# A stick-breaking attention layer with a SwiGLU FFN: first-stage and attention orders joined, two x blocks loaded a projection sooner, xn by tiles, first FFN casts reordered

## The chip, the cores and the metric

The kernel runs on one core of a Trainium2 chip. The metric is device time in microseconds (us) for one launch, taken as the median of several runs. The core has a matmul engine (TensorE, PE in the profile, with its weight loads as PEld), VectorE (DVE), ScalarE (ACT), GpSimd (POOL) and SyncE (SP), which here issues the DMA transfers. Each engine works through its own queue in order. Matmuls write into PSUM, which has eight banks of 128 × 512 float32; everything else lies in SBUF.

## What is computed

One transformer layer, S = 2048 tokens, D = 1024, 16 heads of 64, all float32: a stick-breaking attention, then a SwiGLU feed-forward network. Both are wrapped in RMS norms with shift, scale and gate that come from a conditioning vector c.

```python
mod_all = einsum('bd,lde->lbe', silu(c), ada_w) + ada_b[:, None]
sh_m, sc_m, gt_m, sh_f, sc_f, gt_f = split(mod_all[i][:, None, :], 6, axis=-1)
h = rms_norm(x, norm_g[i, 0]) * (1 + sc_m) + sh_m
q, k, v = heads(h @ w_qkv)
for q0 in range(0, s, 128):                      # stick-breaking attention
    z = einsum('bthd,bshd->bhts', q[:, q0:q0+128], k[:, :q0+128]) * 64 ** -0.5
    sp = where(mask, softplus(z), 0.0)
    a = exp(where(mask, z - cumsum(sp, axis=3, reverse=True), -inf))
    o = einsum('bhts,bshd->bthd', a, v[:, :q0+128])
x = x + gt_m * rms_norm(o @ w_o, norm_g[i, 1])
h = rms_norm(x, norm_g[i, 2]) * (1 + sc_f) + sh_f
g, u = split(h @ ffn_w_in, 2, axis=-1)
x = x + gt_f * rms_norm((silu(g) * u) @ ffn_w_out, norm_g[i, 3])
```

## The kernel before

**Matmuls.** A float32 product is made of three fp32r matmuls on high and low halves: each operand is cast (`high`), the rest is subtracted (`low`), and `mm3` (L160 to L162) adds three of the four products of halves into the same PSUM tile. So every operand needs a cast and a subtraction on other engines before PE may use it, and a tile of h or of a weight appears in the profile as two operations (`ht` with L722 or L348 the cast, L727 or L350 the low half).

**Blocks.** Tokens go in four blocks of 512 (indices 0 to 3; "token blocks 3 and 4" are indices 2 and 3), channels of D in eight slices k of 128 (KC = 8), heads in eight pairs p. A projection step (p, b) makes the keys, queries and values of one pair for one block: three products of eight slices each, in the order t = 1 (keys), 0 (queries), 2 (values). `STEPS` lists the steps; (1, 0) is pulled to the second place and its results are parked in memory (`k_park`, `q_park`, `v_park`), so that the list begins (0, 0), (1, 0), (0, 1), (0, 2), (0, 3). `project` is a generator: it yields after each slice, and the attention slots (scores z, the scan w, the transposes t, the outputs o) are emitted between the slices. After a product, `split` makes high and low of the result (`kn`, `qn`), and SP stores them to the layouts kt and qt that the scores read.

**First stage (0 to about 50 us).** Block 0's norm needs shift and scale of the first norm, columns of silu(c) @ ada_w. For each quarter q of two channel slices, DVE adds up weight rows (`ada_sum`, tile `asum`, L656 and L659), PE multiplies two of the rows itself (`ada_direct`, L669) and then the sum (`ada_rest`, L676), all into columns of one PSUM tile `acol`; `ada_cols_done` (L684 to L687) makes `shift` and `g_eff` on DVE. Then the transposed tiles xT (`x_turn`, L332) are modulated on ACT (L718), cast (L722), their low half taken on DVE (`low`, L727), and three products (keys, queries, values of step (0, 0)) take them slice by slice (`first_products`). The weights w0, w1, w2 of step (0, 0) are cast on ACT (`weights_high`, L697), their low halves made on DVE (`weights_low`, L702).

**x of the other blocks.** Blocks 1 to 3 are loaded by `x_load` (four tiles of 128 tokens, L314), squared on ACT with the mean on DVE and the power on POOL (`x_square`), scaled on DVE into `xn` (`x_scale`, L323), transposed (L332) and modulated slice by slice in `first_norm`. For blocks 2 and 3 the load is emitted at the first slice of the key product of the step just before the block's own. All four squares come at slices 0 to 3 of the following query product, all four scales at slices 4 to 7. Three transposed tiles follow at slices 2, 4 and 6 of the value product, and the other five in the block's own key product. Block 0 and 1 take a PSUM bank of the pool `tps` for xT, blocks 2 and 3 one of the three banks of `accps`, in which the projections' accumulators (`pj`), the turned values (`vt`) and the late modulation's columns (`ap`) rotate. A tile takes the next bank and waits until the tile that had it before is read.

**Late modulation.** `late_modulation` for segments 2, 3 and 4 (the attention's gate, shift and scale of the second norm) runs beside the attention, a little per slot: loads, sums on DVE, then a tile `ap` from `accps`, matmuls (L230, L283) and a result on DVE (L238, L297).

**FFN.** Its two products are done by a scheme with seven block products, whose operands are sums of blocks with high and low halves of their own. `FIRST_AT` says at which product of the first group which left and right operands are split (`left_split`, `right_split`); these casts run on ACT ahead of or behind the copies of the products (L1329).

Of the kernel before, what the change touches and what calls it, by code (L numbers as in the profile page):

```python
# [9 lines left out]
F32 = mybir.dt.float32  # L10
F32R = mybir.dt.float32r
AF = mybir.ActivationFunctionType
ALU = mybir.AluOpType
# [3 lines left out]
P = 128  # L17
D = 1024
S = 2048
KC = D // P  # L20
# [71 lines left out]
def hybrid_trunk_kernel(  # L92
# [83 lines left out]
    def sb(shape, dtype, **kw):  # L176

        return (odd if kw["tag"] in ODD_TAGS else att).tile(shape, dtype, **kw)
# [66 lines left out]
            g_eff[:, which, ks], sc, 1.0, gc[:, which, ks], op0=ALU.add, op1=ALU.mult  # L245
        )

    def late_modulation(segs, tag, n, ahead, waits, pool, ptag, acc_tag="tmp", rows_tag="wraw", settle=3, pace=1):

        chunks = [(seg, half, k0) for seg in segs for half in range(2) for k0 in range(0, KC, n)]  # L250
        loaded = []

        def load():
            if len(loaded) < len(chunks):
                loaded.append(ada_load(*chunks[len(loaded)], n, tag, BUFS[tag]))

        for _ in range(ahead):
            load()
        for at, (seg, half, k0) in enumerate(chunks):
            if ahead == 0 or at == 0:  # L260
# [12 lines left out]
            if k0 + n < KC:  # L273
                continue
            for _ in range(settle):
                yield
            ps = pool.tile([P, BT], F32, name=f"ap{seg}_{half}", tag=ptag)
            if seg in (2, 5):
                g = seg // 3
                rows = sb([P, 2, BT], F32, name=f"gr{g}_{half}", tag=rows_tag, bufs=BUFS[rows_tag])  # L280
                nc.sync.dma_start(rows, gate_consts[g : g + 1, half].to_broadcast((P, 2, BT)))
                if seg == 2:
                    nc.tensor.matmul(ps, ones, acc, start=True, stop=True)  # L283
# [38 lines left out]
    def x_scale(b, i):  # L322
        nc.vector.tensor_scalar(  # L323
            x_norm[b, i], x_tiles.pop((b, i)), x_rstd.pop((b, i)), None, op0=ALU.mult
        )

    def x_turn(b, k):

        pool, tag = (tps, "t") if b < 2 else (accps, "acc")
        pt = pool.tile([P, BT], F32, name=f"xT{b}_{k}", tag=tag)  # L330
        for i in range(4):
            nc.tensor.transpose(  # L332
                pt[:, i * P : (i + 1) * P], x_norm[b, i][:, k * P : (k + 1) * P], ident
            )
        return pt
# [22 lines left out]
        return h  # L358

    norm_h, norm_tile = {0: []}, {}  # L360

    def first_norm(b, k):
        if b is None or k >= KC:
# [29 lines left out]
    def project(at):  # L393
# [3 lines left out]
        early, parked = (p, b) in EARLY, (p, b) == PARKED  # L397

        nb = STEPS[at + 1][1] if at + 1 < len(STEPS) and STEPS[at + 1][0] == 0 else None
        if STEPS[at] == (PARKED[0], 1):  # L400
            unpark()
        h = norm_h[b] if p == 0 or parked else h_load(p, b)

        def product(t):
            if begun:
                return first_acc[t]
            w = weights[p, t]
            if parked and t == 1:
                acc = zps.tile([P, BT], F32, name=f"pj{p}_{b}_{t}", tag="z")
            else:  # L410
                acc = accps.tile([P, BT], F32, name=f"pj{p}_{b}_{t}", tag="acc")
            ahead = b == NB - 1 and p + 1 < NPAIR
            for k in range(KC):
                if t == 1:
                    if p == 0:
                        first_norm(b, k + 3)
                    if k == 0 and nb and nb > 1:
                        x_load(nb)
                    if k == 5 and waiting:
                        waiting.pop()()  # L420
                if parked and t == 1 and k % 2 == 0:
                    nc.sync.dma_start(*stores[k // 2])
                if parked and (t, k) == (1, 6):
                    split_early(1, 2, ["whl"])
                if t == 0 and nb:
                    (x_square if k < 4 else x_scale)(nb, k % 4)
                if t == 2 and k in (2, 4, 6):
                    first_norm(nb, k // 2 - 1)
                if ahead and k == 0:
                    load_weights(p + 1, t)  # L430
                if ahead and k == 6:
                    split_weights(p + 1, t)
                mm3(acc, (w[0][:, k], w[1][:, k]), (h[k][:, 0], h[k][:, 1]), k == 0, k == KC - 1)
                yield
            return acc

# [208 lines left out]
            chunks[q, k] = w[:, :, k % 4]  # L645

    def ada_begin(q):
        cols_ps[q] = zps.tile([P, BT], F32, name=f"acol{q}", tag="z")
        nc.vector.memset(cols_ps[q][:, :4], 0.0)

    def ada_sum(q, k):
        w, scale = chunks[q, k], c_act[:, k : k + 1]
# [13 lines left out]
    def ada_direct(q, k):  # L666

        for n, seg, js in COLUMNS:
            nc.tensor.matmul(  # L669
                cols_ps[q][:, n : n + 1], chunks[q, k][:, seg, js], c_act[:, k : k + 1],  # L670
                start=False, stop=False, skip_group_check=True,
            )

    def ada_rest(q):
        for n, seg, js in COLUMNS:
            nc.tensor.matmul(  # L676
                cols_ps[q][:, n : n + 1], piece_sums[q][:, seg, js], ones[:, 0:1],
                start=False, stop=n == 3, skip_group_check=True,
            )

    def ada_cols_done(q):

        ps, ms = cols_ps.pop(q), slice(2 * q, 2 * q + 2)
        nc.vector.tensor_tensor(shift[:, 0, ms], ps[:, 0:2], b_cols[:, 0, ms], op=ALU.add)  # L684
        sc = sb([P, KC], F32, name=f"sc0_{q}", tag="sc", bufs=1)[:, :2]
        nc.vector.tensor_tensor(sc, ps[:, 2:4], b_cols[:, 1, ms], op=ALU.add)
# [78 lines left out]
    ada_direct(0, 0)  # L765
    turned_x = {m: x_turn(0, m) for m in range(2)}
    ada_direct(0, KC - 1)
    ada_rest(0)
    weights_high(1)
    weights_low(1)  # L770
    ada_cols_done(0)
    weights_high(0)
    weights_low(0)
    weights_high(2)
    full_high(0)
    low(0)
    full_high(1)
    weights_low(2)
    low(1)


    for q in range(4):
        m = 2 * q
        if q < 3:
            if q == 0:
                ada_begin(1)
            begun = 2 if q > 0 else 0
            for n, k in enumerate(ada_sums(q + 1)[begun:]):
# [12 lines left out]
        if q < 3:  # L801
            turned_x[m + 2] = x_turn(0, m + 2)
            ada_direct(q + 1, KC - 1)
            if q == 0:
                first_products(m + 1, (1,))
            turned_x[m + 3] = x_turn(0, m + 3)
            ada_rest(q + 1)
            first_products(m + 1, (0, 2) if q == 0 else (1, 0, 2))
            ada_cols_done(q + 1)
            full_high(m + 2)  # L810
            full_high(m + 3)
# [6 lines left out]
            load_weights(1, 2, "v")  # L818
    split_early(1, 1, ["aT", "aT"])
    split_early(1, 0, ["aT", "aT"])  # L820
    late = late_modulation((2, 3, 4), "wraw", 2, 0, 3, accps, "acc")


    tasks = []
# [544 lines left out]
    def taken(n, product, banks_of):  # L1369
# [256 lines left out]
```

## Time and profile before

| | us |
|---|---|
| median of 3 runs | 2842.39 (2840.52 to 2842.96) |
| profiled execution | 2840.56 |
| its span | 2838.8 |
| PE busy | 2794.5 |
| DVE, ACT, POOL busy | 2023.9, 1632.6, 1281.7 |

The profiled execution's own time is the time that a run of it reports; the span is what the trace covers of it, from the first to the last instruction. The stages by the trace: first stage and parked projection to about 62 us, attention with the other projections to about 1400, the out-projection to about 1550, the FFN's first product to about 2100, its second to the end. In the rows a line such as "PE pj L160 <- DVE qn L440" is a wait: the matmul of line 160 that writes pj stood idle until DVE's operation of line 440 on qn had ended. In the rows of a timeline the bracket at the end is the idle time just before the first instruction of the row, and what ended it. A name is that of a tile without its number, and L is the line of the kernel before.

### The profile page before, as it was taken

To read this page: it belongs to the slowest core of one execution; us is meant where nothing else is said; L and a number is where in the kernel's file an instruction comes from. 1 tells how busy PE (TensorE), PEld (TensorE's weight loads), DVE (VectorE), ACT (ScalarE), POOL (GpSimd) and SP (SyncE) were. 2 spreads that over 40 slices of the span, in tenths; PEclk is the share of its full clock that TensorE was granted. 3 is DMA by queue.
4 is the path that set the end of the run, shared out by engine and by line. 5 is a ranking of instruction groups with operands and counts; after the bars stand their busy time and mean duration, and the time that the engine had idled before them with its cause. 6 is when DMAs were issued, how large, how long until landed. Compare 5 with 4: busy or idle time off the path is not lost.

```text
span 2838.8 us, 41815 instructions
## 1 busy us (share of the span) xinstructions
PE 2794.5 (98%) x13848; PEld 2333.9 (82%) x13848; DVE 2023.9 (71%) x2824; ACT 1632.6 (58%) x3267; POOL 1281.7 (45%) x2032
## 2 busy tenths in 40 slices
PE   7999999999999999999999999999999999999998
PEld 6788888888888888887888888888888888888887
DVE  6788898888888888888866866555776655134367
ACT  5787877788777877877645533333433333322243
POOL 1475666666576655656410222221222222544455
PEclk9999999999999999999999999999999999999999
DMA  8765546657565635636289645325453335545575
GB/s 328 273 211 168 189 151 232 211 169 237 181 212 194 200 125 176 206 123 238 74 302 318 212 135 156 122 89 157 148 171 115 112 106 165 192 136 154 180 231 187
DMA packets 239368, 516.84 MB, mean 182 GB/s; under 512 B 22320, under 2 KB 110384, under 8 KB 221488
## 3 DMA queue, kind: packets, MB, share of 16 engines
q1 hardware_dynamic: 239152, 514.18, 56.0%
q8 instruction: 109, 1.79, 0.3%
q14 instruction: 107, 0.88, 0.1%
HBM read 346.85 MB, written 118.49 MB: 164 GB/s over the span
## 4 chain that ended last, share of the span: by engine, by line
PE 88%; DVE 5%; DMA 3%; ACT 2%; issue 2%; POOL 0%; SPq 0%; DVEq 0%; POOLq 0%; ACTq 0%
PE s L160 9%; PE s L162 9%; PE s L161 9%; PE z L536 8%; PE o L615 8%; PE t L587 8%; PE pj L160 6%; PE pj L161 6%; PE pj L162 6%; PE o L160 5%; PE o L162 5%; PE o L161 5%; PE y L162 1%; PE y L160 1%; PE y L161 1%
## 5 line engine op out<-in xcount | busy, mean ns | idle before, releaser
L577 POOL TENSOR_TENSOR a<-a,w 128x512 f32<-128x512 f32 (+3 forms) x640 | 619.6, 968 | 218.1 <-DVE w L570 127.2
L570 DVE TENSOR_TENSOR_SCAN w<-z,c,begin 128x512 f32<-128x512 f32 x384 | 489.5, 1279 | 81.2 <-ACT z L555 60.9
L160 PE MATMUL s<-r,l 128*128 128x512 f32 x1232 | 480.5, 390 | 1.2 <-ACT p L1329 0.6
L162 PE MATMUL s<-r,l 128*128 128x512 f32 x1232 | 479.5, 389 | 0.0
L161 PE MATMUL s<-r,l 128*128 128x512 f32 x1232 | 479.3, 389 | 0.0
L553 ACT ACTIVATE a<-z 128x512 f32<-128x512 f32 (+3 forms) x640 | 347.0, 542 | 167.5 <-PE z L536 136.0
L615 PE MATMUL o<-aT,v 128*128 128x512 f32 (+3 forms) x1280 | 384.2, 381 | 0.1
L603 DVE TENSOR_TENSOR aT<-t,aT 128x512 fp32r<-128x512 f32 (+3 forms) x640 | 359.0, 595 | 23.0 <-ACT aT L597 22.4
L536 PE MATMUL z<-kt,qt 128*128 128x512 f32 (+3 forms) x1280 | 363.1, 365 | 0.0
L597 ACT CAST aT<-t 128x512 fp32r<-128x512 f32 (+3 forms) x640 | 314.0, 533 | 73.7 <-PE t L587 63.5
L555 ACT ACTIVATE z<-z 128x512 f32<-128x512 f32 (+3 forms) x640 | 345.4, 540 | 0.0
L1393 POOL TENSOR_TENSOR one<-p,p 128x512 f32<-128x512 f32 x44 | 70.5, 1603 | 573.4 <-issue 303.1
L160 PE MATMUL pj<-ht,w 128*128 128x512 f32 x768 | 309.8, 403 | 7.6 <-ACT ht L722 2.6
L161 PE MATMUL pj<-ht,w 128*128 128x512 f32 x768 | 302.1, 393 | 1.2 <-DVE ht L727 0.7
L587 PE MATMUL t<-begin,a 128*128 128x128 f32 x2176 | 294.8, 273 | 8.5 <-DVE aT L603 7.2
L587 PEld LDWEIGHTS t<-begin,a 128*128 128x128 f32 x2176 | 255.1, 140 | 58.1 <-DVE aT L603 11.0
L162 PE MATMUL pj<-ht,w 128*128 128x512 f32 x768 | 302.1, 393 | 0.0
L160 PEld LDWEIGHTS s<-r,l 128*128 128x128 f32 x1232 | 231.2, 188 | 50.4 <-DVE p L1385 1.2
L162 PEld LDWEIGHTS s<-r,l 128*128 128x128 f32 x1232 | 231.2, 188 | 48.3 <-DVE l L1249 0.4
L161 PEld LDWEIGHTS s<-r,l 128*128 128x128 f32 x1232 | 231.3, 188 | 48.0
L565 DVE TENSOR_TENSOR_SCAN w<-z,begin 128x128 f32<-128x128 f32 (+3 forms) x256 | 208.7, 818 | 75.0 <-ACT z L555 62.2
L536 PEld LDWEIGHTS z<-kt,qt 128*128 128x128 f32 x1280 | 230.2, 188 | 37.4 <-DVE w L565 0.2
(164 smaller groups left out, 4865.8 us busy)
## 6 DMA issues: line engine op xcount, KB each, us to landing
ht<-h_s SPq DMA_DIRECT2D x108, 1024.0 KB, 8.1
wi<-in_win SPq DMA_DIRECT2D x86, 512.0 KB, 4.0
qt<-qn SPq DMA_DIRECT2D x124, 256.0 KB, 4.7
ol_qt<-act_s SPq DMA_DIRECT2D x56, 512.0 KB, 3.7
act_s<-S SPq DMA_DIRECT2D x66, 256.0 KB, 4.2
br<-in_wout SPq DMA_DIRECT2D x66, 256.0 KB, 3.5
h_s<-ht SPq DMA_DIRECT2D x16, 1024.0 KB, 7.8
o_s<-os SPq DMA_DIRECT2D x128, 128.0 KB, 2.6
```

The costliest lines, as they stand in the source:

```text
L160: nc.tensor.matmul(acc, lhs[0], rhs[0], start=first, stop=False, **kw)
L161: nc.tensor.matmul(acc, lhs[0], rhs[1], start=False, stop=False, **kw)
L162: nc.tensor.matmul(acc, lhs[1], rhs[0], start=False, stop=last, **kw)
L536: nc.tensor.matmul(z[:, :n], q[:, e, part, r * P : (r + 1) * P], k[:, e, :n], start=part == 0, stop=part == 1,)
L553: nc.scalar.activation(a[:, :n], z[:, :n], AF.Sigmoid, scale=QK_SCALE)
L555: nc.scalar.activation(z[:, :n], z[:, :n], AF.Sigmoid, scale=-QK_SCALE)
L570: nc.vector.tensor_tensor_scan(rest[:, rev], left[:, rev], begin[:, :BT][:, rev], initial=carries[r], op0=ALU.mult, op1=ALU.bypass,)
L577: nc.gpsimd.tensor_tensor(a[:, :n], a[:, :n], rest[:, 1 : n + 1], op=ALU.mult)
L587: nc.tensor.transpose(pt[:, rb * P : (rb + 1) * P], weighed[i, rb][:, j * P : (j + 1) * P], ident)
L597: nc.scalar.copy(hl[:, 0, t0:], pt[:, t0:])
L603: nc.vector.tensor_tensor(hl[:, 1, t0:], pt[:, t0:], f32(hl[:, 0, t0:]), op=ALU.subtract)
L615: nc.tensor.matmul(acc[:, t0:], lhs, hl[:, part, t0:], start=sc == qb and j == 0 and part == 0, stop=sc == 0 and j == 3 and part == 1,)
```

## The change

Five edits.

1. *First stage.* For q = 0 the columns lie in two PSUM tiles, one for each channel slice, and `ada_rest` and `ada_cols_done` can be called for one slice alone. The order at the start is written anew: w1's cast and low half, columns of slice 0, w0's cast, the first tile's modulation and cast, w0's low half, columns of slice 1, the second tile's modulation and cast, the first tile's low half, w2's cast, two of the sums for the next quarter, the second tile's low half, w2's low half. For the quarters after, `ada_rest` comes ahead of the second transposed tile instead of behind it.
2. *Loads of x.* Blocks 2 and 3 are loaded at the second slice of the value product of the step two before the block's own.
3. *xn by tiles.* The scales of tiles 0 and 1 are emitted between the squares (`X_STEPS`); for blocks 2 and 3 four transposed tiles, instead of three, are emitted in the value product, at slices 3 to 6.
4. *Late modulation.* Segments 2, 3 and 4 take their PSUM tile only when the projection's last slice was one of 1 to 4 (`mid_product`).
5. *FFN.* `FIRST_AT` sets five of the first group's splits one or two products later.

```diff
+            while not calm():
+                yield
             ps = pool.tile([P, BT], F32, name=f"ap{seg}_{half}", tag=ptag)
...
+    X_STEPS = {
+        0: [(x_square, 0)], 1: [(x_square, 1)], 2: [(x_scale, 0), (x_square, 2)], 3: [(x_scale, 1)],
+        4: [(x_square, 3)], 5: [(x_scale, 2)], 6: [(x_scale, 3)],
+    }
...
+    place = [0]
+    def mid_product():
+        return 1 <= place[0] <= 4
...
+        b2 = STEPS[at + 2][1] if at + 2 < len(STEPS) and STEPS[at + 2][0] == 0 and at > 0 else None
...
                 if t == 1:
-                    if p == 0:
+                    if p == 0 and (b < 2 or k > 0):
                         first_norm(b, k + 3)
-                    if k == 0 and nb and nb > 1:
-                        x_load(nb)
...
+                if t == 2 and k == 1 and b2:
+                    x_load(b2)
                 if t == 0 and nb:
-                    (x_square if k < 4 else x_scale)(nb, k % 4)
-                if t == 2 and k in (2, 4, 6):
+                    for fn, i in X_STEPS.get(k, ()):
+                        fn(nb, i)
+                if t == 2 and nb and nb > 1:
+                    if k >= 3 and k < 7:
+                        first_norm(nb, k - 3)
+                elif t == 2 and k in (2, 4, 6):
                     first_norm(nb, k // 2 - 1)
...
                 mm3(acc, (w[0][:, k], w[1][:, k]), (h[k][:, 0], h[k][:, 1]), k == 0, k == KC - 1)
+                place[0] = k
                 yield
...
     def ada_begin(q):
-        cols_ps[q] = zps.tile([P, BT], F32, name=f"acol{q}", tag="z")
-        nc.vector.memset(cols_ps[q][:, :4], 0.0)
+        cols_ps[q] = []
+        for j in range(2 if q == 0 else 1):
+            ps = zps.tile([P, BT], F32, name=f"acol{q}_{j}", tag="z")
+            nc.vector.memset(ps[:, :4], 0.0)
+            cols_ps[q] += [ps] * (1 if q == 0 else 2)
...
-    def ada_rest(q):
+    def ada_rest(q, tiles=(0, 1)):
         for n, seg, js in COLUMNS:
+            if n % 2 in tiles:
...
-    def ada_cols_done(q):
-        ps, ms = cols_ps.pop(q), slice(2 * q, 2 * q + 2)
-        nc.vector.tensor_tensor(shift[:, 0, ms], ps[:, 0:2], b_cols[:, 0, ms], op=ALU.add)
+    def ada_cols_done(q, first=0, end=2):
+        ps, ms = cols_ps[q][first], slice(2 * q + first, 2 * q + end)
+        nc.vector.tensor_tensor(shift[:, 0, ms], ps[:, first:end], b_cols[:, 0, ms], op=ALU.add)
...
-    ada_rest(0)
+    ada_rest(0, (0,))
     weights_high(1)
     weights_low(1)
-    ada_cols_done(0)
+    ada_cols_done(0, 0, 1)
+    ada_rest(0, (1,))
     weights_high(0)
+    full_high(0)
     weights_low(0)
+    ada_cols_done(0, 1, 2)
+    full_high(1)
+    low(0)
     weights_high(2)
-    full_high(0)
-    low(0)
-    full_high(1)
+    ada_begin(1)
+    for k in ada_sums(1)[:2]:
+        ada_sum(1, k)
+    low(1)
     weights_low(2)
-    low(1)
...
-                turned_x[m + 3] = x_turn(0, m + 3)
-            ada_rest(q + 1)
-            first_products(m + 1, (0, 2) if q == 0 else (1, 0, 2))
+            else:
+                ada_rest(q + 1)
+                turned_x[m + 3] = x_turn(0, m + 3)
+                first_products(m + 1)
...
-    late = late_modulation((2, 3, 4), "wraw", 2, 0, 3, accps, "acc")
+    late = late_modulation((2, 3, 4), "wraw", 2, 0, 3, accps, "acc", calm=mid_product)
...
     FIRST_AT = {
-        0: [("r", 6)], 2: [("r", 7)], 3: [("l", 7)], 5: [("r", 8)], 7: [("l", 2)], 8: [("r", 9)],
-        9: [("load", 13)], 11: [("l", 4)], 15: [("r", 13)],
+        0: [("r", 6)], 4: [("r", 7)], 5: [("l", 7)], 6: [("r", 8)], 8: [("l", 2)],
+        9: [("r", 9), ("load", 13)], 11: [("l", 4)], 15: [("r", 13)],
     }
```

More of the change, by code (lines that the diff above doesn't have):

```diff
@@ L246, in ada_done, with late_modulation @@
         )
-    def late_modulation(segs, tag, n, ahead, waits, pool, ptag, acc_tag="tmp", rows_tag="wraw", settle=3, pace=1):
+    def late_modulation(segs, tag, n, ahead, waits, pool, ptag, acc_tag="tmp", rows_tag="wraw", settle=3, pace=1, calm=lambda: True):
         chunks = [(seg, half, k0) for seg in segs for half in range(2) for k0 in range(0, KC, n)]
@@ L669, in ada_direct @@
             nc.tensor.matmul(
-                cols_ps[q][:, n : n + 1], chunks[q, k][:, seg, js], c_act[:, k : k + 1],
+                cols_ps[q][n % 2][:, n : n + 1], chunks[q, k][:, seg, js], c_act[:, k : k + 1],
                 start=False, stop=False, skip_group_check=True,
             )
-    def ada_rest(q):
+    def ada_rest(q, tiles=(0, 1)):
         for n, seg, js in COLUMNS:
[L676 to L679, printed above, removed]
-    def ada_cols_done(q):
-        ps, ms = cols_ps.pop(q), slice(2 * q, 2 * q + 2)
-        nc.vector.tensor_tensor(shift[:, 0, ms], ps[:, 0:2], b_cols[:, 0, ms], op=ALU.add)
-        sc = sb([P, KC], F32, name=f"sc0_{q}", tag="sc", bufs=1)[:, :2]
-        nc.vector.tensor_tensor(sc, ps[:, 2:4], b_cols[:, 1, ms], op=ALU.add)
+            if n % 2 in tiles:
+                nc.tensor.matmul(
+                    cols_ps[q][n % 2][:, n : n + 1], piece_sums[q][:, seg, js], ones[:, 0:1],
+                    start=False, stop=n >= 2, skip_group_check=True,
+                )
+    def ada_cols_done(q, first=0, end=2):
+        ps, ms = cols_ps[q][first], slice(2 * q + first, 2 * q + end)
+        nc.vector.tensor_tensor(shift[:, 0, ms], ps[:, first:end], b_cols[:, 0, ms], op=ALU.add)
+        sc = sb([P, KC], F32, name=f"sc0_{q}_{first}", tag="sc", bufs=1)[:, first:end]
+        nc.vector.tensor_tensor(sc, ps[:, 2 + first : 2 + end], b_cols[:, 1, ms], op=ALU.add)
         nc.vector.scalar_tensor_tensor(
@@ L784, in hybrid_trunk_kernel @@
         if q < 3:
[L785 to L788, printed above, removed]
+            for n, k in enumerate(ada_sums(q + 1)[2:]):
                 ada_sum(q + 1, k)
@@ L805, in hybrid_trunk_kernel @@
                 first_products(m + 1, (1,))
-            turned_x[m + 3] = x_turn(0, m + 3)
-            ada_rest(q + 1)
-            first_products(m + 1, (0, 2) if q == 0 else (1, 0, 2))
+                turned_x[m + 3] = x_turn(0, m + 3)
+                ada_rest(q + 1)
+                first_products(m + 1, (0, 2))
+            else:
+                ada_rest(q + 1)
+                turned_x[m + 3] = x_turn(0, m + 3)
+                first_products(m + 1)
             ada_cols_done(q + 1)
```

## The prediction

> **What bounds the kernel now.** I read the page first: the busy totals and the chain that ended last.
>
> ```profile
> span 2838.8 us, 41815 instructions
> PE 2794.5 (98%) x13848; PEld 2333.9 (82%) x13848; DVE 2023.9 (71%) x2824; ACT 1632.6 (58%) x3267; POOL 1281.7 (45%) x2032
> PE 88%; DVE 5%; DMA 3%; ACT 2%; issue 2%; POOL 0%; SPq 0%; DVEq 0%; POOLq 0%; ACTq 0%
> ```
>
> TensorE is the path: busy 98% of the span, and the change takes no matmul away. All it can win is idle time of PE, 2838.8 − 2794.5 = 44.3 us in the whole kernel. So the second view is the list of PE's waits (us in all, times, longest). These are the rows that the edits touch:
>
> ```profile
> PE xT L332 <- DVE xn L323: 1.5, 5, 0.3
> PE acol L676 <- DVE asum L659: 1.0, 1, 1.0
> PE pj L160 <- ACT ht L722: 2.6, 2, 2.0
> PE pj L161 <- DVE ht L727: 0.7, 3, 0.2
> PE pj L161 <- DVE ht L350: 0.5, 2, 0.3
> PE xT L332 <- DVE qn L440: 1.1, 1, 1.1
> PE pj L160 <- ACT hf L342: 0.9, 1, 0.9
> PE pj L160 <- DVE qn L440: 1.4, 1, 1.4
> PE pj L160 <- issue: 1.4, 1, 1.4
> PE pj L160 <- DVE kn L440: 0.9, 1, 0.9
> PE ap L283 <- DVE v L489: 0.7, 1, 0.7
> PE pj L160 <- DVE shift L238: 0.2, 1, 0.2
> PE s L160 <- ACT p L1329: 0.6, 1, 0.6
> ```
>
> They sum to 13.5 us in 21 breaks. A break costs more than its idle time, because the stream has to refill. The timeline of PE (start, duration, engine, operation, idle before) shows how much, in the first stage:
>
> ```profile
> 20.44 0.79 PE L160 MATMUL pj<-ht,w 128*128 128x512 f32 x1 [2.04 <-ACT ht L722]
> 22.18 0.63 PE L160 MATMUL pj<-ht,w 128*128 128x512 f32 x1
> 22.61 0.63 PE L161 MATMUL pj<-ht,w 128*128 128x512 f32 x1
> 24.18 0.39 PE L162 MATMUL pj<-ht,w 128*128 128x512 f32 x1
> 38.53 0.51 PE L160 MATMUL pj<-ht,w 128*128 128x512 f32 x1
> 39.26 0.50 PE L161 MATMUL pj<-ht,w 128*128 128x512 f32 x1 [0.22 <-DVE ht L727]
> 39.59 0.39 PE L162 MATMUL pj<-ht,w 128*128 128x512 f32 x1
> 39.82 0.39 PE L160 MATMUL pj<-ht,w 128*128 128x512 f32 x1
> ```
>
> Two undisturbed starts lie 39.82 − 39.59 = 0.23 us apart. From 38.53 to 39.59 there are 1.06 us for two of them, so this break cost 1.06 − 0.46 = 0.60 us, of which 0.22 was idle: 0.38 of refill at the worst, and I take 0.3. The ceiling of the whole change is then 13.5 + 21 × 0.3 = 19.8 us; a time below 2821 can't come from these waits.
>
> **Part 1, the first stage.** Two columns of shift and gain are made and used before the other two, and w2's cast and low part go behind the four casts of the first two transposed tiles. The rows of DVE and ACT there:
>
> ```profile
> 18.44 0.16 DVE L684 TENSOR_TENSOR shift<-acol,b_cols 128x2 f32<-128x2 f32 x1 [0.87 <-PE acol L676]
> 18.78 1.23 DVE L702 TENSOR_TENSOR w<-wr,w 128x1024 fp32r<-128x1024 f32 x1
> 20.42 0.69 DVE L727 TENSOR_TENSOR ht<-hf,ht 128x512 fp32r<-128x512 f32 x1 [0.41 <-ACT ht L722]
> 21.03 1.22 DVE L702 TENSOR_TENSOR w<-wr,w 128x1024 fp32r<-128x1024 f32 x1
> 27.91 0.48 DVE L656 TENSOR_SCALAR asum<-ac,c_act 128x512 f32<-128x512 f32 x1
> 17.92 1.04 ACT L697 CAST w<-wr 128x1024 fp32r<-128x1024 f32 x1 [0.22 <-DMA wr<-in_wqkv]
> 19.77 0.62 ACT L722 CAST ht<-hf 128x512 fp32r<-128x512 f32 x1
> ```
>
> DVE was idle 0.87 us until PE had all four columns at 18.44. With only the first pair needed I let it go on at 17.55, right after w1's low part (16.35 + 1.23): 0.89 us earlier. On ACT the cast of w2 (1.04) leaves its place before the first tile's. Walking both queues with these durations, the first tile's cast ends at 19.50 instead of 20.39, and DVE, which paces the stage up to the next column sums, ends them at 27.07 instead of 27.98. The three small DVE operations and one memset that are added cost some 0.3 us and stand in DVE's idle time before 20.42 (0.41). PE's wait for the sums (1.0, at 28.03) and the two breaks after it at 31.12 and 31.85 move with DVE's chain: **−0.9 us**. Bounds: 0, if the sums stay where they are (their last input lands by DMA), and −1.3, the 0.9 plus one refill of the 31.85 break.
>
> For q = 1, 2 the column sums go ahead of one transposed tile, so PE reaches them 0.45 us sooner (four transposes) and the modulation behind them starts as much sooner. The three breaks on a low half (L727, 0.2 idle each) have two in this place, 39.26 and 46.62; 0.45 covers 0.22: **−1.0 us**, bounds 0 and −1.2 (two of 0.60).
>
> The cold clock matters for the start. From 20.44 to 24.18 starts are 22.61 − 22.18 = 0.43 us apart, afterwards 0.23: 3.7 us of half rate. The Trainium skill (TensorE: Matmul & The Clock Gate, "The HAM clock gate") says that the first 3.4 us or so of activity run at half clock, by a free-running window and not by a count of matmuls; the 3.7 us here agree. By that rule an earlier first matmul need not bring an earlier end of the cold stretch. In my sum this changes nothing, because PE has 1.0 us of idle before 28.03 to take it up; what a missed window would cost is rival B.
>
> **Parts 2 and 3, x of blocks 2 and 3.** The list has five waits of transposes for xn, 1.5 us idle. One is in block 1, four in block 2, where the loads come last. From the timeline, squares and scales on ACT and DVE, SP's issues, and the score that first reads qt of block 1:
>
> ```profile
> 83.00 1.06 ACT L151 ACTIVATE xn<-x 128x1024 f32<-128x1024 f32 x1 [0.24 <-DMA x<-in_x]
> 84.26 2.74 DVE L323 TENSOR_SCALAR xn<-x,n_rstd 128x1024 f32<-128x1024 f32 x4
> 72.70 3.12 SPq L314 DMA_DIRECT2D x<-in_x x4
> 77.44 0.32 SPq L491 DMA_DIRECT2D v_park<-v x1
> 89.41 3.54 SPq L470 DMA_DIRECT2D qt<-qn x4
> 106.22 0.33 PE L536 MATMUL z<-kt,qt 128*128 128x128 f32 x2
> ```
>
> The same 10 us by windows (length, busy time of PE, PEld, DVE, ACT and POOL with counts, PE clock, DMA share, GB/s), and two rows of the DMA issues from 60 to 130 us (count, size, us to landing):
>
> ```profile
> 80.00:90.00 10.00, 8.85 (x43) 6.89 (x43) 4.85 (x10) 5.30 (x10) 2.89 (x5) 1.00 1.01 388
> x<-in_x SPq DMA_DIRECT2D x8, 512.0 KB, 7.8
> v_park<-v SPq DMA_DIRECT2D x1, 512.0 KB, 13.2
> ```
>
> ACT's last square starts at 83.00 behind its load; the four scales (0.69 each) run after all squares, and PE transposes as each comes. The four loads now stand in SP's queue right behind q's parking store, some 4 to 7 us sooner, and xn0 and xn1 are scaled before the last squares. All five breaks should go: 1.5 + 5 × 0.3 = 3.0 at most, **−2.5 us** (I leave 0.5, since the last tile is still scaled late). Block 2's tail, the two breaks on L350 (0.5 + 2 × 0.3 = 1.1), comes from that same lateness; I take **−0.7**, with 0.2 of new waits for a bank taken off, bounds 0 and −1.1. In block 3 the waits of 1.1 (transposes behind qn) and 0.9 (a product behind a transposed tile in its bank) are 2.6 with refills. The four transposed tiles now come one per step in the value product, which moves both; but a cast that ran in a quiet stretch moves into one where DVE and GpSimd work, and a transposed tile follows another in one bank. I take **−0.5**, bounds −2.6 and +1.5. Four scales more or less cost nothing by themselves: DVE works 4.85 of 10 us there (80 to 90).
>
> The moved loads cost in SP's queue. Three of block 3's tiles now stand ahead of the stores that make qt of block 1. One waits for v_park to land (77.44 + 13.2 = 90.6; before, qt was issued at 89.41: +1.2), and 1.5 MB at the 388 GB/s of the window are 3.9 us. The four copies took 7.9 us to land (97.3 then), so now 102.4, and the first score that reads them is at 106.22: 3.8 us of cover, less about 1 that the gains in between take. So nothing, but with thin cover: every us beyond 2.8 costs PE one. Bounds 0 and +3. The two weight loads that drop behind kt are first cast at 147, with 40 us to spare: nothing.
>
> **Part 4, the late modulation.** Its tile takes one of three banks that the projections' accumulators rotate through, and the list has five waits at those places: qn 1.4, no named releaser 1.4, kn 0.9, v 0.7, shift 0.2, together 4.6 us, with refills of 0.2 (the long ones hide a part) 5.6. Starting only inside a product (steps 1 to 4) changes the rotation from then on. By the order in which tiles are taken, these five pairs part, and three new pairs meet with nothing between: a product on the bank of the key product two before, one behind a late column, a transposed tile behind a cast. The nearest rows price the first two at 0.9 to 1.4 + 0.3 each, the third at 0.5; they may also be just in time. I take 2.9 of the 0 to 3.9: **−2.7 us**, bounds −5.6 and 0 (further meetings that I did not see).
>
> **Part 5, the FFN's first casts.** PE waits 0.6 for the cast of the first products' sum, because four other casts stand ahead of it on ACT. They follow later now: **−0.7**, bounds 0 and −0.9. The casts moved back are wanted some products later, and PE's list has nothing else at L160 on ACT there.
>
> **Sum.** 0.9 + 1.0 + 2.5 + 0.7 + 0.5 + 2.7 + 0.7 = 9.0 us. The profiled execution took 2840.56, of which 1.76 lie outside its span; it becomes 2831.6. The median is 2842.39, 1.83 above it, so **2833.4 us** (−0.32%). All bounds at the good end together (−1.3 −1.2 −3.0 −1.1 −2.6 −5.6 −0.9) are −15.7, at the bad end +4.5 (+3 +1.5).
>
> **The rivals.** *A: half is given back.* PE at 98% runs into the next wait: the bank rotation brings as many new meetings as it parts, and the transposes wait for DVE in place of the loads. For it: the same three banks, and DVE's chain behind every tile. Against: the waits for xn end on a DMA, which does come sooner. With part 4 at 0, block 3 at +0.5 and part 1 at 0.5: 2842.4 − (0.5 + 0.5 + 2.5 + 0.7 − 0.5 + 0.7) = 2838.0. *B: the cold stretch lasts one window more*, 3.4 to 3.7 us: PE then makes 8 matmuls where it would make 16, losing 8 × 0.2 = 1.6, of which the remaining 0.5 of idle takes a part; 2834.5. That is the clock-gate rule's case; one trace can't show how the window lies. *C, slower: qt of block 1 comes late.* The tile waiting for v_park holds SP's queue, and everything behind it with it. The point from which it decides is a landing after 102.4 + 2.7 + 9.0 = 114; SP held to about 109 would put it at 121 and the time at 2833.4 + 15.6 = 2849. For it: DMA engines are full there (1.01). Against: v_park would need some 30 us to land, where it took 13.2. *D: everything on the list that is touched goes,* with no new meeting: −15.7, 2826.7.
>
> **How the numbers follow.** Forecast 0.55, A 0.20, B 0.07, C 0.11, D 0.07. A measurement of this kernel can tell about 0.2%, 5.7 us, from no change: faster means below 2836.7, slower above 2848.1. Faster holds the forecast (own range 2829.5 to 2836.5), B, D and a little of A: 0.70; same is most of A and the upper edge of the others: 0.19; slower is C: 0.11. The range runs from 2826 to 2842, which takes in A, B and D and the bounds of the terms, and leaves C out.
>
> **What would show it.** The first product starts near 19.5 instead of 20.44, and the wait at L676 stays near 1.0. The list of PE's waits has no row of xT behind xn, or one below 0.5 us, and none at L1329. Squares of block 2 don't wait for x. The sum of waits of products in 430 to 1000 us falls from 4.6 to about 2. Wrong would be: a new row of z waiting for qt near 105 (C), rows of pj behind qn or kn as large as before (A), or PE's busy time rising while its waits fall.

## The result, and the profile after

| | kernel before | changed kernel |
|---|---|---|
| median of the comparison | 2842.52 us (2840.33 to 2846.34, 8 runs) | 2832.83 us (2830.58 to 2836.36, 8 runs) |
| profiled execution | 2840.56 | 2832.96 |
| its span | 2838.8 | 2830.6 |

The ratio is 0.9967, with a 95% interval of 0.9956 to 0.9978: the change makes the kernel 9.7 us faster, where 9.0 were forecast (2833.4). The interval excludes no change.

The page of the changed kernel, its first two lines (span; busy time of the engines):

```profile
span 2830.6 us, 41823 instructions
PE 2793.6 (99%) x13848; PEld 2337.3 (83%) x13848; DVE 2020.6 (71%) x2828; ACT 1632.5 (58%) x3267; POOL 1283.8 (45%) x2032
```

PE's busy time is 0.9 us less than before; the other 7.3 of the 8.2 us of span came out of its idle time (44.3 us before, 37.0 now). These rows of PE's waits in the changed kernel (us in all, times, longest) answer the list of before:

```profile
PE h2T L971 <- DVE x1n L964: 2.1, 2, 1.6
PE pj L160 <- DVE kn L464: 2.1, 1, 2.1
PE pj L160 <- ACT ht L751: 1.7, 2, 1.2
PE t L611 <- POOL w L574: 0.8, 1, 0.8
PE pj L160 <- DVE sc L243: 0.5, 1, 0.5
PE xT L341 <- ACT hf L351: 0.4, 2, 0.2
PE pj L161 <- DVE ht L359: 0.3, 1, 0.3
PE pj L161 <- DVE ht L756: 0.2, 1, 0.2
```

Gone are xT behind xn (1.5), acol behind asum (1.0), products behind qn (1.4), behind nothing named (1.4), behind hf (0.9) and shift (0.2), ap behind v (0.7), and the FFN's wait for p (0.6). Not all of this is the edits' doing: in a second trace of the same kernel the wait for asum is back at 0.9, and 0.2 of the wait for p is left; the first trace lacks the wait for asum because its cold stretch lasted longer (below). A product behind kn has grown, 0.9 before, 2.1 now. Two rows are new: a transpose behind GpSimd's w (0.8, at 126.52 us, in block 3) and a product behind sc (0.5). And h2T behind x1n, which no edit touches, rose from 1.1 to 2.1.

PE's timeline in the changed kernel, at the places the forecast named and at the new wait:

```profile
19.73 0.80 PE L160 MATMUL pj<-ht,w 128*128 128x512 f32 x1 [1.18 <-ACT ht L751]
23.19 0.63 PE L161 MATMUL pj<-ht,w 128*128 128x512 f32 x1
24.23 1.05 PE L341 MATMUL xT<-begin,xn 128*128 128x128 f32 x4
26.52 0.39 PE L161 MATMUL pj<-ht,w 128*128 128x512 f32 x1
27.45 1.05 PE L705 MATMUL acol<-ones,asum 128*128 128x1 f32 x8
444.60 0.50 PE L160 MATMUL pj<-ht,w 128*128 128x512 f32 x1 [2.05 <-DVE kn L464]
445.17 0.39 PE L162 MATMUL pj<-ht,w 128*128 128x512 f32 x1
446.09 0.63 PE L162 MATMUL pj<-ht,w 128*128 128x512 f32 x1
448.43 0.63 PE L161 MATMUL pj<-ht,w 128*128 128x512 f32 x1
```

The first product starts at 19.73 instead of 20.44. The wait of 2.05 us at 444.60 is followed by matmuls of 0.63 us, the same duration as in the cold start at 23.19: PE ran at half clock until 449. The windows view of that stretch (length, busy time of PE, PEld, DVE, ACT and POOL with counts, PE clock, DMA share, GB/s) shows the granted clock of 0.50:

```profile
442.10:445.50 3.40, 1.35 (x6) 0.77 (x5) 3.15 (x5) 2.07 (x6) 2.60 (x6) 1.00 0.60 192
445.60:449.00 3.40, 3.40 (x10) 2.75 (x9) 2.07 (x3) 0.69 (x2) 1.68 (x2) 0.50 0.72 236
449.00:452.40 3.40, 3.40 (x23) 3.01 (x22) 2.65 (x4) 2.88 (x7) 1.22 (x2) 1.00 0.73 237
```

The clock-gate section of the Trainium skill that the prediction drew on (TensorE: Matmul & The Clock Gate, "The HAM clock gate") gives 3.4 us as the length of such a window; the stretch here was 3.4 us, so trace and rule agree.

To see where the time went I paired the n-th projection, score, output and FFN matmul of two traces, the same work in both, and took the difference of their starts. All rows are against the trace of the kernel before (us; minus is ahead):

| trace | at 60 | at 160 | at 1200 | at 1500 | at the end |
|---|---|---|---|---|---|
| changed kernel | −1.3 | −6.6 | −8.2 | −8.3 | −8.1 |
| changed kernel, second trace | −1.2 | −6.4 | −9.2 | −9.3 | −9.3 |

So the first stage gave 1.3 us, x of blocks 1 to 3 gave 5.2, the late modulation 1.6 (2.8 in the second trace), and the FFN's gain was taken by the norm in between (h2T). The stretch from 160 to 1200 us isn't the late modulation's alone: the first experiment loses 0.7 us there without it.

### The profile page after: what moved, and what is told of

Same layout as the page of the kernel before. It is cut to its first block, busy times and chain, and to the rows that moved or that the text cites. A ratio compares the mean times of both kernels' runs of the same rounds, so it can differ in the third digit from the quotient of the medians.

```text
span 2830.6 us, 41823 instructions
## 1 busy us (share of the span) xinstructions
PE 2793.6 (99%) x13848; PEld 2337.3 (83%) x13848; DVE 2020.6 (71%) x2828; ACT 1632.5 (58%) x3267; POOL 1283.8 (45%) x2032
## 4 chain that ended last, share of the span: by engine, by line
PE 90%; DVE 4%; DMA 2%; ACT 1%; issue 1%; POOL 1%; SPq 0%; DVEq 0%; POOLq 0%; ACTq 0%
PE s L160 10%; PE s L162 9%; PE s L161 9%; PE z L560 8%; PE o L639 8%; PE t L611 8%; PE pj L160 6%; PE pj L161 6%; PE pj L162 6%; PE o L162 5%; PE o L161 5%; PE o L160 5%; PE y L162 1%; PE y L160 1%; PE y L161 1%
## 5 line engine op out<-in xcount | busy, mean ns | idle before, releaser
L611 PE MATMUL t<-begin,a 128*128 128x128 f32 x2176 | 295.0, 273 | 8.5 <-DVE aT L627 7.0
L611 PEld LDWEIGHTS t<-begin,a 128*128 128x128 f32 x2176 | 255.2, 140 | 58.0 <-DVE aT L627 11.0
```

What stands on the lines that cost most here:

```text
L611: nc.tensor.transpose(pt[:, rb * P : (rb + 1) * P], weighed[i, rb][:, j * P : (j + 1) * P], ident)
```

## Experiments

Medians are compared with the kernel before on the same chip: 2840.88 us (22 runs) for the first four, 2841.78 (8) for the next four, 2841.64 (18) for the last two. Their intervals are about 0.001 wide on each side, 3 us, so single terms are read from the traces, by the differences at the same five places:

| trace | median | ratio to before | at 60 | at 160 | at 1200 | at 1500 | at the end |
|---|---|---|---|---|---|---|---|
| part 4 left out | 2833.72 | 0.9976 | −1.2 | −6.4 | −5.7 | −5.7 | −7.5 |
| part 4, not in the key product | 2830.82 | 0.9964 | +1.8 | −3.5 | −6.1 | −6.1 | −8.0 |
| loads back | 2833.92 | 0.9975 | −1.7 | −3.0 | −6.7 | −6.8 | −7.6 |
| scales back | 2834.49 | 0.9977 | −1.5 | −4.8 | −6.4 | −6.5 | −6.5 |
| part 4, value product only | 2830.92 | 0.9962 | −1.6 | −6.8 | −9.7 | −9.8 | −11.6 |
| first stage back | 2830.90 | 0.9962 | +0.1 | −5.2 | −9.0 | −9.0 | −9.9 |
| FFN order back | 2831.77 | 0.9964 | −1.4 | −6.7 | −9.6 | −9.7 | −9.3 |
| part 4, value product, steps 5 and 6 | 2835.83 | 0.9978 | −1.5 | −6.7 | −5.5 | −5.5 | −5.5 |
| x of blocks 1 to 3 back | 2837.68 | 0.9984 | +2.0 | +2.0 | −0.2 | −0.2 | +0.4 |

### 1. Part 4 left out

```diff
-            while not calm():
-                yield
```

> The changed kernel without part 4 (the late modulation takes its bank at once). Theory: part 4 parts the old pairs but makes a new one, the query product of pair 2 on block 3 behind the keys of the same step (2.05 us idle at 444.6 in the changed kernel), and that idle time then costs a half-clock stretch of 3.4 us (445.6 to 449.0). Expect the break at 444.6 and the half-clock stretch gone, the old waits back near 435 (0.7 idle), 547 (1.4), 864 (1.4) and 964 (0.9), and a span 1 to 2.5 us longer than 2830.6. Rival: the half-clock stretch has nothing to do with the idle time; it stays somewhere between 400 and 500 us, and the span is 3 to 5 us longer.

Its waits have the old rows back, and kn is at its old 0.9:

```profile
PE pj L160 <- issue: 1.4, 1, 1.4
PE pj L160 <- DVE qn L453: 1.4, 1, 1.4
PE pj L160 <- DVE kn L453: 0.9, 1, 0.9
PE ap L283 <- DVE v L502: 0.7, 1, 0.7
```

The 2.05 us wait at 444 is gone, and no half-clock stretch lies after 32 us until the kernel's end (one lies in the first stage, from 28.20 to 31.61). From 160 to 1200 us it lost 0.7 us against the kernel before, where the changed kernel gained 1.6: part 4 is worth 2.3 us in a trace with the half-clock stretch, 3.5 in one without. The span is 0.7 us longer than the changed kernel's, a little under the expected 1 to 2.5, since its norm before the FFN waited 0.6 us and not 2.1. The theory holds; the rival (the stretch stays, 3 to 5 us) falls.

### 2. Part 4, other places

The first try forbids the key product, the second allows the value product alone, the third only its steps 5 and 6:

```diff
-        return 1 <= place[0] <= 4
+        return place[1] != 1 and 1 <= place[0] <= 4
...
+        return place[1] == 2 and 1 <= place[0] <= 4
...
+        return place[1] == 2 and 5 <= place[0] <= 6
```

> The changed kernel with part 4 allowing the late modulation's bank only in the query and value products, not in the key product. Theory: a bank taken inside the key product, where the turned values take one too, sends the query product onto the bank of the keys just made. Then the 2.05 us wait for kn near 444.6 is gone, with it the half-clock stretch (about 1.7 us), and the wait for sc near 870 (0.5) too: span 3.5 to 4.5 us shorter than 2830.6. Rival: other pairs meet on the three banks instead and cost as much: span within 1.5 us of 2830.6, with rows of products behind kn, qn or ht of 1 us and more in 430 to 1000 us.

The wait at 444 was gone, but the span was 2830.8, as long as the changed kernel's. Two things hide in that. Its first stage ran cold until 35.9 us, so PE was 1.8 us behind at 60, where the changed kernel was 1.3 ahead: 3.1 us that part 4 didn't cause. From 160 to 1200 us it gained 2.6 us, against 1.6 and 2.8 of the two traces of the changed kernel. And new meetings stand in its list:

```profile
PE pj L160 <- DVE qn L464: 1.8, 2, 1.0
PE ap L286 <- DVE kn L464: 1.2, 2, 1.1
```

So the rival (meetings move) was right about the list, and the theory about the half-clock stretch alone.

> The changed kernel with the late modulation's bank taken only in the value product (steps 1 to 4). Theory: there the turned values have not taken their bank yet and the next product falls on the bank of the query product made a whole product before, so none of the pairs meets: no wait of a product for kn, qn or sc and none of ap between 430 and 1000 us above 0.3 us, no half-clock stretch after 400 us, span 3 to 4.5 us shorter than 2830.6 (less what the first stage's cold clock takes in that execution), median 2828 to 2830. Rival: meetings only move, as they did when the key product alone was forbidden (2.3 us stayed in 440 to 460): span within 1.5 us of 2830.6.

From 160 to 1200 us this version gained 2.9 us; no half-clock stretch occurred. It ended at 11.6 us ahead, the best trace of all (span 2827.2), 1.7 of it at the norm and the FFN's start. But a row came in for one that left:

```profile
PE pj L160 <- DVE gr L300: 3.6, 2, 2.5
```

A key product now stands on the bank of a column whose reader, on DVE, comes late. Its median is 2830.92 (2829.21 to 2831.34) beside a single 2831.81 of the changed kernel measured with it; the interval, 0.9948 to 0.9976, overlaps that of the changed kernel. The expected 2828 to 2830 was missed.

> The changed kernel with the late modulation's bank taken only at steps 5 and 6 of the value product. Where it was taken at steps 1 to 4 of that product, two products still waited for gr (2.5 and 1.1 us idle), because the pool gave the next key product the bank of a column not yet read. Here no product and no turned values stand behind ap or behind the product just before in the program's list of banks. Theory: no wait of pj above 0.3 us for kn, qn, gr or sc from 430 to 1000 us; the stretch 434 to 1000 is won in full against the kernel before (5.5 us by the forecast's list), span 2825 to 2827 if the first cold stretch ends near 24 us, median 2828 to 2830. Rival: what is won is lost again to waits of transposes, outputs or DMA, and the median stays at 2830.5 to 2832.

A plain miss: 2835.83, slower than the changed kernel and outside both theories. The list of banks had been read for products behind columns and behind the product just before, and not for products behind turned values:

```profile
PE pj L160 <- DVE v L513: 3.7, 2, 2.3
PE pj L160 <- issue: 3.2, 2, 1.8
```

Its timeline at the longest of them:

```profile
471.67 0.50 PE L160 MATMUL pj<-ht,w 128*128 128x512 f32 x1 [2.28 <-DVE v L513]
```

The key product now comes onto the bank of the values turned just before it (2.28 us), and a second such wait (1.40 us) lies near 602. Two more products wait near 729 (1.43) and 859 (1.77) for nothing that the profile names. In every version tried, one tile more on three banks pushed some other tile onto a bank that was still to be read; which one it is decided between 0.5 and 2.5 us of idle time.

### 3. Loads and order of x

Loads back at the first slice of the key product, and, in another kernel, squares ahead of scales:

```diff
-                if t == 2 and k == 1 and b2:
-                    x_load(b2)
...
+                    if k == 0 and nb and nb > 1:
+                        x_load(nb)
```

```diff
-                    for fn, i in X_STEPS.get(k, ()):
-                        fn(nb, i)
+                    (x_square if k < 4 else x_scale)(nb, k % 4)
```

> The changed kernel with the loads of x for blocks 2 and 3 at their old place (first slice of the key product of the step before), scales still between the squares. Theory: the early loads remove the waits of block 2's transposes for xn and of block 3's behind them. Expect squares that wait for x again, rows of xT behind xn near 83 to 87 us with 1.0 to 1.6 us idle, and a span 2 to 4 us longer than 2830.6. Rival: the order by tiles does it, and the loads matter less than 1 us; then at most 0.5 us of idle of xT behind xn and a span within 1 us.

> The changed kernel with all four squares ahead of the four scales again, loads still early. Theory (the loads do it): xT behind xn stays below 0.6 us idle in block 2, span within 0.8 us of 2830.6, and only block 1's two breaks (0.9 us with refill) come back. Rival (the order by tiles does it): four breaks of block 2's transposes for xn come back, 1.2 us idle, and the span is 2 to 3.5 us longer.

Loads back: only one break of block 2's transposes came back (0.4 us idle), so for these breaks the rival was right and the order by tiles is enough. But PE was 3.6 us worse at 160 (−3.0 against −6.6), from another place. Timeline of the kernel with the loads back, ACT first, then PE:

```profile
103.74 1.06 ACT L151 ACTIVATE xn<-x 128x1024 f32<-128x1024 f32 x1 [2.11 <-DMA x<-in_x]
104.79 0.46 ACT L621 CAST aT<-t 128x384 fp32r<-128x384 f32 x1
105.90 0.48 PE L611 MATMUL t<-begin,a 128*128 128x128 f32 x1 [2.39 <-DVE aT L627]
```

ACT's square waits 2.11 us for x of block 3; the attention's cast aT stands behind it in ACT's queue, DVE behind that cast, and PE waits 2.39 us for DVE. After it came a half-clock stretch (below). In the changed kernel the squares of block 2 start at 76.31 and those of block 3 at 101.25, and none of them waits for x. So the early loads aren't worth much for block 2's transposes; here they would have kept a late load from blocking the attention's own work. In the kernel before, with the loads in the same place, the same square starts at 106.21 without a wait, so this is the case of one trace, and how often it comes isn't shown. At the end the span was only 0.6 us longer than the changed kernel's, inside the rival's bound: this trace had no half-clock stretch near 445 and gained 3.7 us from 160 to 1200, where the changed kernel gained 1.6. Its median is 1.1 us above the changed kernel's, which the intervals can't tell apart.

Scales back, loads early: only block 1's breaks came back (0.3 us idle; 0.24 + 0.55 with refill), none in block 2, as the theory had it. The trace is 1.8 us behind at 160, of which 0.8 are block 1; the rest comes in block 3, where DVE scales later. The bound of 0.8 us on the span was missed (1.7). For block 2 either edit alone removes all or nearly all of the breaks: the two are not a sum.

### 4. x of blocks 1 to 3 back

The loads, squares, scales and transposes as before, the other parts changed.

> The changed kernel with the loads, the squares and scales and the transposes of x in blocks 1 to 3 as they were before. Theory: parts 2 and 3 together are worth 5.2 us by the first trace (60 to 160 us), more than the 3.7 of the forecast, because block 3's tail gains 1.6 and not 0.5. Expect PE 5 us behind the changed kernel at 160 us, waits of xT behind xn of 1.5 us idle, and a span 4 to 6 us longer. Rival: the gain at 160 us was that execution's only; then the loss is 2 to 4 us, as the forecast had it.

```profile
PE xT L335 <- DVE xn L326: 1.3, 4, 0.3
PE xT L335 <- DVE qn L451: 1.1, 1, 1.1
PE pj L160 <- ACT hf L345: 0.9, 1, 0.9
PE pj L161 <- DVE ht L353: 0.6, 2, 0.3
```

The rows of before are back, xn with 1.3 us in 4 waits instead of 1.5 in 5. From 60 to 160 us this trace gained nothing (+2.0 to +2.0), the changed kernel 5.2 and 5.3. The median is 4.9 us above the changed kernel's 2832.83. The theory holds: 5.2 us and not 3.7. Of the span, 8.5 us longer than the changed kernel's where 4 to 6 were expected, some 3 us are a longer cold start (below).

### 5. First stage back, FFN order back, and a second trace

> The changed kernel with the first stage as it was before. Theory: the joined order is worth 1.3 us (0.6 by the column sums, 0.35 at each of the two breaks near 39 and 46 us). Expect PE's waits for asum (1.0) and the two waits for ht (0.2 each) back, and PE behind the changed kernel by 1.3 us at 60 us, if the clock comes up at the same time. Rival: the first stage is set by when the clock comes up to full speed, and the order is worth nothing: no difference at 60 us beyond the difference of the cold stretches.

At 60 us this trace stands at +0.1, the two of the changed kernel at −1.3 and −1.2: the joined order is worth 1.3 us, with the cold stretch ending at 24.6 here and at 25.7 and 23.8 there. So between these three traces it isn't set by the clock. But at the end this trace was 9.9 us ahead, more than either of the changed kernel, and its median 2830.90 can't be told from it. Of the lead of 1.3, only 0.2 is left at 1200 us against the second trace (−9.0 to −9.2), and what took it between 160 and 1200 isn't shown; the rest is the norm and the FFN's start, where it gained 0.9 while the second trace lost 0.2.

> The changed kernel with the first FFN casts in the old order. Theory: only the break near 1566 us (idle 0.6, 0.8 to 0.9 with refill) comes back, so the median is within 1.5 us of the changed kernel's. Rival: the casts moved back make new waits later, and the old order is as fast or faster by 0.3 us in the stretch from 1560 to 1700.

At 2831.77 it can't be told from the changed kernel. Where the old order stands the FFN's wait came back only half (0.3 us idle), perhaps because the norm's h2T had kept PE back just before (1.4 us); with the new order 0.2 us of it stood in the second trace. In the first trace of the changed kernel the FFN's start gained 0.9 us and h2T lost 1.0. Nothing in this case shows what makes h2T wait longer at one time than at another beyond this: ACT's cast ahead of it waits for a load of r from memory, 1.94 us before and 2.71 in the changed kernel's first trace, and that load is not among the edits.

> The changed kernel once more, with another trace. Theory: the half-clock windows are 3.41 us long and free-running, so their phase differs: the end of the first cold stretch moves between 23 and 27 us, and the stretch after the 2.05 us wait near 444.6 comes only if most of the wait falls into one window. Rival: the end of the cold stretch and the second stretch are fixed by the work, and come at 25.7 and 445.6 again to 0.2 us.

The same wait, the other outcome. Windows of the second trace of the changed kernel, then of the kernel with the scales back:

```profile
440.17:443.58 3.41, 2.47 (x12) 1.51 (x10) 2.63 (x3) 3.41 (x9) 3.41 (x5) 1.00 0.05 18
443.59:447.00 3.41, 2.16 (x10) 1.84 (x11) 3.38 (x7) 0.83 (x2) 2.05 (x5) 1.00 0.88 291
447.00:450.40 3.40, 3.40 (x23) 2.96 (x22) 2.74 (x4) 2.85 (x6) 1.36 (x3) 1.00 0.66 221
```

```profile
443.00:446.40 3.40, 1.25 (x5) 0.73 (x5) 3.13 (x5) 2.92 (x8) 3.12 (x6) 0.99 0.39 132
446.40:449.70 3.30, 3.30 (x8) 2.72 (x9) 3.02 (x4) 0.00 (x0) 2.01 (x4) 0.50 0.85 262
```

In the second trace of the same kernel the wait (2.10 us at 444.84) fell across two windows of 3.4 us, PE was busy 2.47 and 2.16 us in them, and the clock stayed at 1.00. Windows are laid here by the clock's own changes in the trace, every 3.413 us. Where PE was busy 1.35 and 1.25 us in one window (and 1.41 in the kernel with the loads back, at 102, and 1.45 in the one with x back, at 449), the next ran at 0.50. Where it was busy 1.63 (steps 5 and 6, at 857) or 2.00 (FFN order back, at 440), it didn't. Seven traces have this wait, 2.05 to 2.10 us long; three of them a half-clock stretch behind it. The theory holds: the phase decides, and it is dear: from 436 to 460 us the first trace lost 4.0 us of its lead, the second 2.5.

## Why the prediction was right

**What bounds.** PE's idle time gave 7.3 of the 8.2 us; busy time fell by 0.9. The ceiling of 19.8 us was not near. That the sum came out so close is partly luck, because errors in its terms cancel: in the first trace part 1 came out 0.6 us short, x 1.5 over, part 4 1.1 short, and h2T, which the sum doesn't have, took 1.0.

**Part 1** was over-sized: −1.9 forecast, −1.3 measured. The breaks at 39 and 46 us lost their idle time but not all of their refill, 0.37 each where 0.5 each were taken; the column sums on DVE ended at 27.40 where 27.07 was forecast and 27.98 stood before, 0.6 earlier and not 0.9. Half of what was missing is that trace's own: its first load landed 0.16 later (PE's wait for it was 11.7 instead of 11.6 us, and w1's low half began at 16.51 instead of 16.35), which the sum had taken as fixed (its walk starts from 17.55, where 16.35 + 1.23 gives 17.58). The order of the queues came out as walked: shift at 17.74, the first low half at 19.71 instead of 20.42.

**Parts 2 and 3** were under-sized: −3.7 forecast, −5.2 measured, twice and by the kernel without them. Block 1 and 2's breaks were 2.8 where 2.5 were taken, block 2's tail 0.85 for 0.7. Block 3 was the mis-sized term: −1.6 for −0.5, because the loss set against it (2.1 us for a cast that moves beside GpSimd's work and for a bank) was too large: the one new wait there is the transpose behind GpSimd's w, 0.79 us. Both of its waits, 1.1 behind qn and 0.9 behind hf, went, inside the bound of −2.6. The split between loads and order was wrong: each removes block 2's breaks, or all but one, without the other, and what the loads add, by the one trace without them, is a free queue of ACT for block 3.

**SP's queue** (rival C) behaved as worked out, with more cover. In the changed kernel the issues and the load of the scores' keys and queries are these:

```profile
63.20 4.58 SPq L317 DMA_DIRECT2D x<-in_x  x4
80.59 8.53 SPq L317 DMA_DIRECT2D x<-in_x  x3
89.18 4.58 SPq L494 DMA_DIRECT2D qt<-qn  x4
101.26 0.33 PE L560 MATMUL z<-kt,qt 128*128 128x128 f32 x2
```

The three tiles of block 3 hold SP for 8.53 us, as the waiting v_park made them, and qt goes out at 89.18, where 90.6 was forecast and 89.41 was before. No score waits for it: rows of z behind a DMA are missing from the list.

**Part 4** was right in sum and by luck in parts: −2.7 forecast, −1.6 and −2.8 measured in the two traces, or −2.3 and −3.5 against the kernel without it. All five old waits went, and the waits of products from 430 to 1000 us fell from 4.6 to 2.5 where about 2 was forecast. One of the forecast's own signs of being wrong came all the same: a row behind kn, larger than before. Of the new meetings, the product behind kn took 2.05 us where 0.9 to 1.4 were taken from the nearest rows, the one behind the late column 0.5. What no row of before showed is the price behind a long wait: half of a 3.4 us window, 1.7 us (the two traces, one with it and one without, differ by 1.5 there). The picture of a rotation was too simple. The outputs o take their banks from the same pool (L611 of the kernel before), which the description above leaves out. By the program's list of banks, which no trace here shows, the pool doesn't hand them out in turn; that would be why three attempts to place the column better moved the meeting and didn't remove it.

**Part 5** gave 0.9 at its own place in the first trace (0.7 forecast) and nothing that the end of the run shows.

**Rival B** was the right mechanism at the wrong place and size. In the changed kernel's first trace the cold stretch ended at 25.7 instead of 24.0 and cost nothing, because the sums' wait took it up, as the forecast said. In two kernels it lasted to 36 us; three rows of PE in the one with x back, the third at full rate again:

```profile
33.08 0.63 PE L160 MATMUL pj<-ht,w 128*128 128x512 f32 x1
35.64 0.63 PE L160 MATMUL pj<-ht,w 128*128 128x512 f32 x1
36.38 0.39 PE L162 MATMUL pj<-ht,w 128*128 128x512 f32 x1
```

There PE was some 2.3 us behind the kernel before at 30 us, where the changed kernel's first trace was 0.6 ahead: a longer cold start can cost 3 us and not the 1.1 to 1.6 of the rival. Two of the ten traces with the new first stage have it and neither of the two with the old one; that is too few to say whether the new order brings it more often, and no run tests it. It may be, with the stretch at 445, a part of the 5.8 us between the fastest and the slowest run of the changed kernel; that isn't shown, as those runs have no trace.

## What to carry to other kernels

Where PE is at 98%, list its waits by what ended them and price each break with its refill; a change can only win what stands there, and it wins terms that are not independent, such as an early load and a finer order that remove the same break. A load that comes late can hurt through the engine that waits for it: look at what stands behind the waiting instruction in its queue, here the attention's cast behind a square. A wait over half a clock window may cost its own length and half a window more, and by chance, so remove the longest waits first.

## What the runs showed of the hardware that was not expected

One wait of 2.05 us, with PE busy 1.35 of 3.40 us in a window, brought the clock to 0.50 for the next 3.4 us; 1.63 to 2.00 us did not. The cold start can last much longer than one window: with the first product at 19.63 us, one kernel was at half rate until 36.2, 16.6 us, though PE's rows leave little idle time in between. The clock column reads 1.00 in that stretch; there the granted clock isn't recorded, and the matmuls' distance (0.43 or 0.23 us) has to be read instead. "The warm-up budget is ~3.4 µs of time, not a number of matmuls" (the Trainium skill, TensorE: Matmul & The Clock Gate, "The HAM clock gate") fits the 3.7 us of the kernel before and not these 16.6 us.

Busy time as the rows count it doesn't decide alone. The windows of the kernel without part 4 show this, with PE busy 3.18 of 3.42 us and half clock right after:

```profile
24.78:28.20 3.42, 3.18 (x25) 2.75 (x23) 3.28 (x7) 0.00 (x0) 0.00 (x0) 1.00 1.13 362
28.20:31.61 3.41, 3.41 (x10) 2.65 (x10) 3.23 (x8) 2.59 (x4) 0.00 (x0) 0.50 1.03 423
```

This window holds many matmuls for acol, which are one column wide. If they are left out of the count, the windows of all twelve traces part (from the first matmul to 2815 us). The five at full clock that half clock followed had 1.23 to 1.64 us of other matmuls, and no other window at full clock had less than 1.63. Windows at half clock were followed by full clock from 2.96 us on, and up to 2.95 by another at half clock. That the chip leaves such matmuls out isn't shown; it fits these traces, and no run tested it.
